# Two layers of a hybrid trunk on one core: what is worked around the last gates, and the passage from layer 0 to layer 1

## The chip, the core and the metric

The kernel runs on one core of a Trainium2 chip. A core has the engines TensorE (PE: matmuls), VectorE (DVE), ScalarE (ACT), GpSimd (POOL) and SyncE (SP, which here only issues DMAs), each with an instruction queue of its own that it works in order, and 16 DMA engines that carry all its transfers. The metric is the device time of one execution in microseconds (us).

## The reference

Two layers work on 256 latent tokens and 256 context tokens of width 1024. Layer 1 gives no context output, so its second half has 256 tokens where layer 0 has 512.

```python
def trunk_layer(x, xc, ...):
    pl = split_cols(modulate(rmsnorm(x, n1_g), sh1, sc1) @ w_in)     # and pc from xc
    ya, yb, yc = gdn_mixer(...), diff_mixer(...), natten_mixer(...)
    x = x + gt1 * merge_branches(ya, yb, yc, pl[12], w_up, w_out)
    x = x + gt2 * peer_ffn(modulate(rmsnorm(x, n2_g), sh2, sc2), p_wq, p_keys, p_u, p_v)

def peer_ffn(h, wq, keys, u, v):            # 8 heads, 128 x 128 experts, 16 kept per head
    s = einsum('thpd,hpnd->thpn', (h @ wq), keys)
    sv, si = top_k(s, 16); ...; top_s, top_pos = top_k(cand_s, 16)
    gate = softmax(top_s)                    # idx: the 16 experts of each head
    act = gelu(einsum('td,thkd->thk', h, u[idx]))
    return einsum('thk,thkd->td', gate * act, v[idx])
```

## The kernel before

The Tile framework's scheduler fixes the order in each engine's queue when the kernel is built; `tc.issue_after(x)` puts an instruction behind x. Activations are feature-major: partitions hold features, columns hold tokens. A matmul in full precision is three passes over high and low parts (`mm3`, L240 to L246); `wload` (L213) brings a weight tile by DMA, ACT makes the high part, DVE or POOL the low part.

**PEER** is worked densely over the experts, in 128 tiles by the first key's index i1. For each i1 there is a *u stage* (24 matmuls of `mm3` over the tile of u, Gelu at L1325), a product with the gates `Gt` (DVE, L1326), a split into `ah` (ACT, L1330) and `al` (DVE, L1331), and a *V stage* (`vstage`, L1294: for each block of 128 tokens six matmuls of 512 columns into PSUM banks that collect over all i1). The tiles of v are loaded and split beforehand (`vparts`, L1303 and L1305; L158 and L159). In layer 0 the 384 tokens of blocks 1 to 3 go this way, 18 matmuls in a V stage; in layer 1 256 tokens, 12 matmuls. Block 0 of layer 0 goes by gathers: POOL fetches rows of u and v by indirect DMA (L1256), DVE forms the dot products (L1262) and the sum `gacc` (L1274). `due` (L1289) deals 260 such items over the i1: from GA on, over GB tiles, twice as many for i1 below 16 and for 26 to 111 as for the others (`share`).

**The gates.** `spread` (L1198) builds the table of gates by groups c of four tokens, 96 of them in layer 0 and 64 in layer 1: DVE (one c in eight: ACT) makes one-hot matrices (L1207, L1210, L1215), PE multiplies them (L1218), ACT copies the result to `stg` (L1219). Each 32 tokens are written to `Gd` in DRAM (L1224) and read back as `Gt`, four i1 at a time (L1314). Between the groups PE gets other work: `early_tiles` (L1167) works the first 26 u tiles in plain fp32 (L1176, eight matmuls or *fills* each), eleven of them before the gates and fifteen among them, as evenly as `fill` (L1188) can spread them: 120 fills over the 96 or 64 groups.

**From layer 0 to layer 1.** The residual is written to DRAM as `xs2` (L1010) after layer 0's second norm and comes back as `xr0` (L1346). `gacc` is transposed and added at i1 = 120 (L1347); after the last V stage the sums are copied (L1364, L1366), transposed (L1371) and added (L1374). Layer 1 then takes the sums of squares (L165 to L173), normalises all 512 columns (`norm_mod`, L178 to L207) and works its first projection tiles 4, 5, ..., whose convolutions follow.

## Time and profile before

| | us |
|---|---|
| median of three runs (3756.0, 3765.81, 3756.54) | 3756.54 |
| the profiled execution: its time / its span | 3751.19 / 3749.4 |
| busy: PE, DVE, ACT, POOL | 3549.1, 2710.7, 1553.2, 988.5 |

The span is the time from the first to the last instruction in the trace. Busy times overlap, since the engines work beside each other. The granted clock of PE is 1.00 at its upper level of 2.4 GHz, and 0.50 at the lower one of 1.2 GHz; a figure between is a mean over a stretch.

### The profile page before, as it was taken

How to read it: one execution, taken by the hardware profiler on the slowest of the kernel's cores; microseconds unless marked ns; L12 is line 12 of the kernel's file. 1: busy time of each engine (PE TensorE's matmuls, PEld its weight loads, DVE VectorE, ACT ScalarE, POOL GpSimd, SP SyncE). 2: the span in 40 equal slices, each digit the busy share in tenths (PEclk: the TensorE clock that was granted, in tenths of full speed). 3: DMA queues.
4: the chain of work that ended last, by engine and by line, in shares of the span. 5: the costliest groups of instructions: out<-in, count | busy, mean ns of one | idle time of the engine just before them, and what ended most of it. 6: DMA issues, size and time to landing. Idle time of an engine off the chain costs nothing. (4 is left out here: it accounts for less than half of the span.)

```text
span 3749.4 us, 53254 instructions
## 1 busy us (share of the span) xinstructions
PE 3549.1 (95%) x19889; PEld 3052.4 (81%) x19889; DVE 2710.7 (72%) x5479; ACT 1553.2 (41%) x2454; POOL 988.5 (26%) x761
## 2 busy tenths in 40 slices
PE   7899999898999889999999989998999999999998
PEld 4788766677778679999999977887698998999997
DVE  7767556975999777777777648687567886666666
ACT  4312554224347433333333334123655475444444
POOL 3311332333300344433443212121333100222221
PEclk9989999999999999999999999799999999999999
DMA  4211123652235899888888732224245468666664
GB/s 183 97 43 33 47 76 117 219 171 94 87 135 208 318 335 317 295 296 310 291 301 300 251 115 85 74 92 162 72 148 163 146 237 265 211 211 206 216 213 132
DMA packets 265587, 681.56 MB, mean 182 GB/s; under 512 B 20976, under 2 KB 115696, under 8 KB 261744
## 3 DMA queue, kind: packets, MB, share of 16 engines
q1 hardware_dynamic: 228464, 543.93, 43.4%
q0 software_dynamic: 36864, 134.23, 10.3%
q8 instruction: 156, 2.56, 0.3%
q14 instruction: 103, 0.84, 0.1%
HBM read 626.17 MB, written 51.90 MB: 181 GB/s over the span
## 5 line engine op out<-in xcount | busy, mean ns | idle before, releaser
L246 PE MATMUL pm<-hhi,wlo 128*128 128x256 f32 (+2 forms) x2888 | 968.8, 336 | 22.0 <-DVE wlo L229 19.8
L244 PE MATMUL pm<-hhi,whi 128*128 128x256 f32 (+2 forms) x2888 | 968.9, 336 | 16.0 <-ACT whi L227 12.8
L245 PE MATMUL pm<-hlo,whi 128*128 128x256 f32 (+2 forms) x2888 | 970.4, 336 | 1.3 <-POOL hlo L207 0.9
L227 ACT CAST whi<-wr 128x1024 fp32r<-128x1024 f32 (+1 forms) x430 | 430.3, 1001 | 865.8 <-PE pm L245 672.4
L246 PEld LDWEIGHTS pm<-hhi,wlo 128*128 128x128 f32 x2888 | 554.2, 192 | 64.9 <-DVE wlo L229 26.6
L244 PEld LDWEIGHTS pm<-hhi,whi 128*128 128x128 f32 x2888 | 554.8, 192 | 61.2 <-ACT whi L227 13.6
L245 PEld LDWEIGHTS pm<-hlo,whi 128*128 128x128 f32 x2888 | 554.7, 192 | 47.4 <-issue 5.2
L232 POOL TENSOR_TENSOR wlo<-wr,whi 128x1024 fp32r<-128x1024 f32 x124 | 300.7, 2425 | 1086.6 <-ACT whi L227 1032.5
L1300 PE MATMUL ps<-vh,ah 128*128 128x512 f32 x1280 | 401.0, 395 | 22.2 <-ACT ah L1330 13.8
L1300 PE MATMUL ps<-vl,ah 128*128 128x512 f32 x1280 | 398.9, 393 | 0.9 <-DVE vl L159 0.9
L1300 PE MATMUL ps<-vh,al 128*128 128x512 f32 x1280 | 397.9, 392 | 0.2 <-DVE al L1331 0.2
L159 DVE TENSOR_TENSOR vl<-vr,vh 128x1024 fp32r<-128x1024 f32 x256 | 313.6, 1225 | 89.9 <-ACT vh L158 89.6
L232 DVE TENSOR_TENSOR wlo<-wr,whi 128x1024 fp32r<-128x1024 f32 x181 | 223.7, 1236 | 197.1 <-ACT whi L227 196.7
L158 ACT CAST vh<-vr 128x1024 fp32r<-128x1024 f32 x256 | 268.5, 1049 | 175.2 <-PE ps L1300 107.7
L1256 POOL DMA_INDIRECT gr<-in_un_dram,gix x128 | 175.5, 1371 | 476.6 <-DVE gr L1262 231.2
L1326 DVE TENSOR_TENSOR act<-act,Gt 128x384 f32<-128x384 f32 (+1 forms) x256 | 222.2, 874 | 103.8 <-ACT act L1325 91.2
L1300 PEld LDWEIGHTS ps<-vl,ah 128*128 128x128 f32 x1280 | 241.2, 189 | 56.4 <-DVE vl L159 3.6
L1300 PEld LDWEIGHTS ps<-vh,al 128*128 128x128 f32 x1280 | 241.2, 189 | 53.1 <-DVE al L1331 0.8
L1300 PEld LDWEIGHTS ps<-vh,ah 128*128 128x128 f32 x1280 | 233.4, 190 | 61.3 <-ACT ah L1330 16.5
L1330 ACT CAST ah<-act 128x384 fp32r<-128x384 f32 (+1 forms) x256 | 117.2, 459 | 385.2 <-DVE act L1326 365.6
L1176 PE MATMUL pm<-h2f,wr 128*128 128x384 f32 (+1 forms) x832 | 251.4, 433 | 2.8 <-ACT act L1179 2.8
L1256 POOL DMA_INDIRECT gr<-in_v_dram,gix x128 | 177.6, 1387 | 279.5 <-DVE gacc L1274 239.3
(386 smaller groups left out, 5619.6 us busy)
## 6 DMA issues: line engine op xcount, KB each, us to landing
wr<-in_u_dram SPq DMA_DIRECT2D x256, 512.0 KB, 4.6
vr<-in_v_dram SPq DMA_DIRECT2D x256, 512.0 KB, 4.7
wr<-in_w_in_dram SPq DMA_DIRECT2D x130, 512.0 KB, 3.6
aw<-in_ada_w_dram SPq DMA_DIRECT2D x88, 512.0 KB, 4.3
Gd<-stg SPq DMA_DIRECT2D x20, 2048.0 KB, 7.2
Gt<-Gd SPq DMA_DIRECT2D x32, 768.0 KB, 7.6
wr<-in_wq_dram SPq DMA_DIRECT2D x32, 512.0 KB, 3.5
Gt<-Gd SPq DMA_DIRECT2D x32, 512.0 KB, 4.7
```

The source lines that it names most:

```text
L158: (e_hi or ACT.copy)(hi, t)
L159: (e_lo or POOL).tensor_tensor(lo, t, hi, op=OP.subtract)
L227: ACT.copy(hi[:, :k], raw[:, :k])
L232: e.tensor_tensor(lo[:, :k], raw[:, :k], hi[:, :k], op=OP.subtract)
L244: PE.matmul(p, whi[:, i, :], xhi[:, i, c0:c1], start=st, stop=False)
L245: PE.matmul(p, whi[:, i, :], xlo[:, i, c0:c1], start=False, stop=False)
L246: PE.matmul(p, wlo[:, i, :], xhi[:, i, c0:c1], start=False, stop=sp)
L1176: e = PE.matmul(p[:, 0:TD], raw[:, k], h2f[:, k, G0:T], start=k == 0, stop=k == 7).ins
L1256: POOL.indirect_dma_start(out=r, out_offset=None, in_=src, in_offset=bass.IndirectOffsetOnAxis(ap=gix[:, j:j + 1], axis=0))
L1300: PE.matmul(acc[t][hf], x1[:, c], x2[:, 512 * hf:512 * hf + 512], start=i1 == 0 and n == 0, stop=i1 == 127 and n == 2)
L1326: DVE.tensor_tensor(a.rearrange("p (b t) -> p b t", t=TB), a.rearrange("p (b t) -> p b t", t=TB), Gt[:, :, e, :], op=OP.mult)
L1330: ACT.copy(ah, a)
```

## The change

- `PRE` gets a fourth number: three of the early u tiles in layer 0 and four in layer 1 (24 and 32 fills) no longer lie between the groups of the gates but behind the last one.
- The first two tiles of v are loaded and split with `wload` before the last 128 tokens' gates, in the buffers of the weights (low part on DVE). The last write to `Gd` is cut in two: the columns of the first eight i1, then the others.
- The gathers start at i1 = 8 (GA) where they started at 2; they end at 120 as before.
- The last three V stages (`LAST`) are put off and worked block by block of tokens at the end.
- In layer 0 each finished block passes to layer 1 token-major: `finish` adds it to the residual, takes the norm's factor and scales; `modulated` transposes it and applies shift and scale. Blocks 0 and 1 pass before layer 1's first matmul; blocks 2 and 3 pass while four projection tiles (4 to 7) are worked on columns 0 to 255, and the same tiles follow on columns 256 to 511. For it `xs2` is written token-major (32 transposes, 8 copies, 8 DMAs behind layer 0's second norm), the gate vector goes to DRAM and back as rows (`g2d`, `g2w`), and layer 1's `xs1` is written by 16 transposes, 4 copies and 4 DMAs behind the four tiles.

```diff
-GA, GB = 2, 118
+LAST = 3
+EARLY1 = ((4, "pa"), (5, "pa"), (6, "pm"), (7, "pm"))
+GA, GB = 8, 112
-PRE = ((16, 10, 11), (26, 0, 11))
+PRE = ((16, 10, 11, 3), (26, 0, 11, 4))
...
             else:
-                DVE.scalar_tensor_tensor(mg, mod[:, 8:16, :], 1.0,
...
-                ready[1, 4] = wload(w_in[1, 4])
-                norm_mod(xT, sumsq(xT, 512), npool, 512, hhi, hlo, mg, mod[:, 0:8, :])
-            if l == 1:
+                parts[:] = [wp, pool(st, "ep", 2)]
+                tiles = [(PSUM(tag), *wload(w_in[1, j])) for j, tag in EARLY1]
+                for c in (0, 256):
+                    for n, (p, whi, wlo) in enumerate(tiles):
+                        e = mm3(p[:, c:c + 256], whi, wlo, hhi, hlo, (c, c + 256))
+                        if c == 0 and n < 2:
+                            with tc.issue_after(e):
+                                modulated(2 + n, xt0[:, 2 + n],
+                                          npool.tile([128, 8, 128], F32, name=nm("nz"), tag="nz", bufs=2), "ps")
+                for (j, _), x in zip(EARLY1, tiles):
+                    early[1, j] = x[0]
+                parts[:] = [wp] * 2
                 xs_dram = dr.tile([128, 8, 256], F32, name="xs1")
-                SP.dma_start(xs_dram, xT[:, :, 0:256])
+                for t in range(2):
+                    for hf in range(2):
+                        p = PS()
+                        for k in range(4):
+                            PE.transpose(p[:, 128 * k:128 * k + 128],
+                                         xt0[:, t, 512 * hf + 128 * k:512 * hf + 128 * k + 128], ident)
+                        w = npool.tile([128, 4, 128], F32, name=nm("nt"), tag="nt", bufs=4)
+                        ACT.copy(w, p.rearrange("p (k n) -> p k n", k=4))
+                        SP.dma_start(xs_dram[:, 4 * hf:4 * hf + 4, 128 * t:128 * t + 128], w)
...
+            if l == 0:
+                xs2 = dr.tile([4, 128, 1024], F32, name="xs2")
+                for t in range(4):
+                    for hf in range(2):
+                        p = PS()
+                        for k in range(4):
+                            PE.transpose(p[:, 128 * k:128 * k + 128], xT[:, 4 * hf + k, 128 * t:128 * t + 128], ident)
+                        w = npool.tile([128, 512], F32, name=nm("nt"), tag="nt", bufs=4)
+                        ACT.copy(w, p)
+                        SP.dma_start(xs2[t, :, 512 * hf:512 * hf + 512], w)
+                g2d = dr.tile([2, 1024], F32, name="g2d")
+                for i in range(2):
+                    SP.dma_start(g2d[i].rearrange("(k p) -> p k", p=128), mod[:, 40:48, i])
         if l == 0:
-            xs2 = dr.tile([128, 8, 512], F32, name="xs2")
-            SP.dma_start(xs2, xT)
...
-                    fill(8 * NR + -(-8 * (NP - NR) * at_[2] // (TD // 4)) - at_[1])
-                SP.dma_start(Gd[(128 // TB) * t + b - G0 // TB], stg)
+                    fill(8 * NR + -(-8 * (NP - NR - NE) * at_[2] // (TD // 4)) - at_[1])
+                g = Gd[(128 // TB) * t + b - G0 // TB]
+                if at_[2] < TD // 4:
+                    SP.dma_start(g, stg)
+                else:
+                    for c in (slice(0, 2 * GS), slice(2 * GS, 128)):
+                        SP.dma_start(g[:, c], stg[:, c])
+                    fill(8 * NE)
...
+                if t == NT - 1:
+                    vready = {}
+                    for i1 in range(2):
+                        vh, vl = wload(v[l, i1].rearrange("p (k n) -> p k n", k=8), e=DVE)
+                        vready[i1] = [x.rearrange("p k n -> p (k n)") for x in (vh, vl)]
                 spread(t, rt_[t])
...
-                if i1:
+                if i1 > 0 and i1 <= 128 - LAST:
                     vstage(*acts.pop(0))
...
+                    SP.dma_start(xt0, xs2.rearrange("t p n -> p t n"))
...
+            def finish(b, parts_):
+                y, i = xt0[:, b], b // 2
+                w = dp.tile([128, 1024], F32, name=nm("gr"), tag="gr", bufs=4)
                 for hf in range(2):
+                    c = slice(512 * hf, 512 * hf + 512)
+                    DVE.tensor_tensor(w[:, c], parts_[hf], g2w[:, i, c], op=OP.mult)
+                    DVE.tensor_tensor(y[:, c], y[:, c], w[:, c], op=OP.add)
+                    ACT.activation(w[:, c], y[:, c], AF.Square, accum_out=ss[:, b, hf:hf + 1])
+                DVE.tensor_tensor(ss[:, b, 0:1], ss[:, b, 0:1], ss[:, b, 1:2], op=OP.add)
+                r = rstd_cols(dp, ss[:, b, 0:1], 1, 1.0 / D, EPS)
...
+                ACT.activation(yn[:, 0:512], y[:, 0:512], AF.Copy, scale=r)
+                DVE.tensor_scalar(yn[:, 512:1024], y[:, 512:1024], r, None, op0=OP.mult)
+                return yn
+            def modulated(b, yn, z, tag):
...
+                        last["norm"] = ACT.activation(z[:, d], p[:, 128 * k:128 * k + 128], AF.Identity, scale=mg1[:, d, i:i + 1],
+                                                      bias=mods[1][:, d, i:i + 1]).ins
+                    DVE.tensor_copy(hhi[:, h, n], z[:, h])
+                    DVE.tensor_tensor(hlo[:, h, n], z[:, h], hhi[:, h, n], op=OP.subtract)
+            for b in range(NTB + 1):
+                for x in acts if b else ():
+                    vstage(*x, ts=(b - 1,))
+                yn = finish(b, acc[b - 1] if b else [gacc[:, 0:512], gacc[:, 512:1024]])
+                if b < 2:
+                    modulated(b, yn, dp.tile([128, 8, 128], F32, name=nm("gr"), tag="gr", bufs=4), "pm")
+        else:
+            for t in range(NTB):
+                for x in acts:
+                    vstage(*x, ts=(t,))
```

The end of layer 0's gates in PE's queue, before: L1218 are the products of a group, L1176 a fill with its early tile `pm`, and L244 to L246 the u stage of i1 = 26, with which the stage of experts begins.

```order
L1218 MATMUL ps_10174<-o_2167_10181,o_2166_10175 128x128
L1218 MATMUL ps_10174<-o_2168_10184,o_2166_10175 128x128
L1218 MATMUL ps_10174<-o_2169_10187,o_2166_10175 128x128
L1218 MATMUL ps_10174<-o_2170_10190,o_2166_10175 128x128
L1176 MATMUL pm_10086<-h2f_6790,wr_10084 128x384
L244 MATMUL pm_11106<-hhi_6779,whi_11102 128x384
L245 MATMUL pm_11106<-hlo_6780,whi_11102 128x384
L246 MATMUL pm_11106<-hhi_6779,wlo_11103 128x384
```

And after, where L1249 are the products of a group, L1206 a fill, and L1344 the V stage of i1 = 0:

```order
L1249 MATMUL ps_10213<-o_2181_10223,o_2179_10214 128x128
L1249 MATMUL ps_10213<-o_2182_10226,o_2179_10214 128x128
L1249 MATMUL ps_10213<-o_2183_10229,o_2179_10214 128x128
L1206 MATMUL pm_10109<-h2f_6790,wr_10107 128x384
L1206 MATMUL pm_10240<-h2f_6790,wr_10238 128x384 x8
L1206 MATMUL pm_10253<-h2f_6790,wr_10251 128x384 x8
L1206 MATMUL pm_10266<-h2f_6790,wr_10264 128x384 x8
L1344 MATMUL ps_10289<-whi_9639,ah_10298 128x512
```

Three early tiles stand behind the last group, and the V stage follows them; the u stages of i1 = 26 and 27 that stood there now come behind the 25th V stage.

The same place in SP's queue, before: L1224 writes the last part of the gates, L221 loads u tiles, L1314 reads the gates of the first four i1, L1305 loads v tiles.

```order
L221 DMA wr_11100<-in_u_dram 128x1024
L221 DMA wr_11171<-in_u_dram 128x1024
L1224 DMA Gd_6897<-stg_10047 128x4096
L221 DMA wr_11241<-in_u_dram 128x1024
L221 DMA wr_11312<-in_u_dram 128x1024
L1314 DMA Gt_10216<-Gd_6897 128x12x128
L1305 DMA vr_10223<-in_v_dram 128x1024
L1305 DMA vr_10234<-in_v_dram 128x1024
```

And after, where L1203 and L225 load u tiles (the last of these that of i1 = 26), L1261 writes the last part of the gates in two, L1360 reads gates and L1351 loads v tiles:

```order
L1203 DMA wr_10238<-in_u_dram 128x1024
L1261 DMA Gd_6963<-stg_10090 128x256
L1261 DMA Gd_6963<-stg_10090 128x3840
L1203 DMA wr_10251<-in_u_dram 128x1024
L1203 DMA wr_10264<-in_u_dram 128x1024
L225 DMA wr_11129<-in_u_dram 128x1024
L1360 DMA Gt_10295<-Gd_6963 128x12x128
L1351 DMA vr_10330<-in_v_dram 128x1024
L1351 DMA vr_10359<-in_v_dram 128x1024
```

The first `Gt` stands behind three u tiles in place of two, and the first v tile of this stretch is that of i1 = 2.

ACT's queue at the end of layer 0, before: L1330 is the last `ah`, L1366 copies the sums, L165 and L169 square the residual's rows, L227 casts tiles of the input projection.

```order
L1325 ACTIVATE act_18109<-pm_18084 128x384
L1330 CAST ah_18112<-act_18109 128x384
L1366 COPY otm_18158<-ps_10210 128x512
L1366 COPY otm_18186<-ps_10211 128x512
L1366 COPY otm_18158<-ps_10214 128x512
L1366 COPY otm_18186<-ps_10215 128x512
L165 ACTIVATE ssq_18234<-xr_11169 128x512
L169 ACTIVATE ssq_18234<-xr_11169 128x512
L227 CAST whi_18392<-wr_18390 128x1024
L227 CAST whi_18480<-wr_18478 128x1024
L169 ACTIVATE ssq_18234<-xr_11169 128x512
```

And after, behind the scaling of block 3: L231 casts the weight tiles 5, 7, 8 and on, L1436 applies shift and scale to blocks 2 and 3, L391 copies `xs1`; the hand-over of the first projection tile to its convolution comes behind the fourth such copy.

```order
L231 CAST whi_18359<-wr_18357 128x1024
L231 CAST whi_18373<-wr_18371 128x1024
L1436 ACTIVATE nz_18401<-ps_18402,mod_64,mg_18158 128x128 x4
L1436 ACTIVATE nz_18401<-ps_18413,mod_64,mg_18158 128x128 x4
L231 CAST whi_18826<-wr_18824 128x1024
L1436 ACTIVATE nz_18448<-ps_18449,mod_64,mg_18158 128x128 x4
L1436 ACTIVATE nz_18448<-ps_18460,mod_64,mg_18158 128x128 x4
L231 CAST whi_18878<-wr_18876 128x1024
L231 CAST whi_18919<-wr_18917 128x1024
L391 COPY nt_18621<-ps_18616 128x512
L391 COPY nt_18629<-ps_18624 128x512
L391 COPY nt_18637<-ps_18632 128x512
```

The casts of tiles 5 and 7 stand ahead of the modulation of blocks 2 and 3, and four copies of `xs1` stand between the projection tiles and their convolution.

## Rows read from the trace of the kernel before

**Rows 1.** The page: span, then busy time, share and instructions of each engine.

```profile
span 3749.4 us, 53254 instructions
...
PE 3549.1 (95%) x19889; PEld 3052.4 (81%) x19889; DVE 2710.7 (72%) x5479; ACT 1553.2 (41%) x2454; POOL 988.5 (26%) x761
```

**Rows 2.** Windows: stretch, length, busy us of PE, PEld, DVE, ACT, POOL, clock, DMA.

```profile
1074.00:1237.00 163.00, 162.80 (x1007) 131.33 (x1008) 152.10 (x468) 123.20 (x170) 0.00 (x0) 1.00 0.51 190
1254.40:1350.00 95.60, 81.78 (x319) 62.98 (x320) 75.63 (x118) 27.65 (x38) 44.97 (x34) 0.92 0.97 350
1350.00:2200.00 850.00, 848.93 (x4274) 769.79 (x4273) 616.71 (x747) 306.46 (x411) 304.09 (x218) 1.00 0.83 289
```

**Rows 3.** Timeline of PE, last gates of layer 0: start, us, engine, line, operation.

```profile
1234.39 1.05 PE L1218 MATMUL ps<-o,o 128*128 128x128 f32 x8
1235.28 0.81 PE L1176 MATMUL pm<-h2f,wr 128*128 128x384 f32 x2
1235.92 1.05 PE L1218 MATMUL ps<-o,o 128*128 128x128 f32 x8
...
1254.38 1.65 PE L1300 MATMUL ps<-vh,ah 128*128 128x512 f32 x3 [8.43 <-ACT vh L158]
```

**Rows 4.** Timeline of SP's queue at the same place.

```profile
1238.12 0.33 SPq L1224 DMA_DIRECT2D Gd<-stg  x1
1238.55 3.41 SPq L221 DMA_DIRECT2D wr<-in_u_dram  x2
1245.43 0.38 SPq L1314 DMA_DIRECT2D Gt<-Gd  x1
```

**Rows 5.** Waits of PE from 1230 to 1350: total us, times, longest.

```profile
PE ps L1300 <- ACT ah L1330: 12.7, 5, 5.3
```

**Rows 6.** Lines from 1350 to 2200: operands, count, busy us and mean ns, idle before.

```profile
L159 DVE TENSOR_TENSOR vl<-vr,vh 128x1024 fp32r<-128x1024 f32 x109 | 133.6, 1226 | 15.5 <-ACT vh L158 15.4
...
L1262 DVE SCALAR_TENSOR_TENSOR gr<-gr,htm 128x1024 f32<-128x1024 f32 x95 | 115.8, 1219 | 1.8 <-DMA gr<-in_un_dram,gix 1.8
...
L1326 DVE TENSOR_TENSOR act<-act,Gt 128x384 f32<-128x384 f32 x106 | 58.4, 552 | 0.0
...
L1331 DVE TENSOR_TENSOR al<-act,ah 128x384 fp32r<-128x384 f32 x107 | 59.7, 558 | 56.3 <-ACT ah L1330 56.2
```

**Rows 7.** Timeline of PE and ACT at the end of layer 0.

```profile
2216.90 0.63 PE L1300 MATMUL ps<-vh,ah 128*128 128x512 f32 x2
...
2222.35 1.07 ACT L1366 COPY otm<-ps 128x512 f32<-128x512 f32 x2 [3.63 <-PE ps L1300]
...
2225.10 3.03 PE L1371 MATMUL ps<-cst,otm 128*128 128x128 f32 x24
...
2244.27 1.87 PE L173 MATMUL ps<-cst,ssq 128*128 128x1 f32 x8 [16.14 <-DVE ssq L170]
...
2251.18 1.22 PE L244 MATMUL pm<-hhi,whi 128*128 128x512 f32 x2 [2.37 <-DVE hhi L206]
```

**Rows 8.** Windows: first convolutions of layer 1.

```profile
2265.00:2325.00 60.00, 56.35 (x282) 46.56 (x280) 47.55 (x85) 25.92 (x41) 10.65 (x18) 0.94 0.31 97
```

**Rows 9.** Windows: layer 0's second norm, and behind it.

```profile
895.00:907.20 12.20, 5.07 (x14) 2.53 (x15) 10.41 (x23) 11.08 (x20) 5.11 (x3) 0.50 0.57 204
907.20:930.00 22.80, 22.80 (x105) 18.58 (x105) 13.42 (x82) 8.66 (x12) 10.09 (x10) 0.93 0.16 52
```

**Rows 10.** The page, DMA queue: packets, MB, share of 16 engines.

```profile
q1 hardware_dynamic: 228464, 543.93, 43.4%
```

**Rows 11.** Windows: gates of layer 1.

```profile
2975.00:3083.00 108.00, 108.00 (x748) 101.87 (x747) 103.05 (x309) 83.01 (x119) 2.77 (x1) 1.00 0.58 211
```

**Rows 12.** Timeline of PE behind those gates.

```profile
3096.31 0.58 PE L244 MATMUL pm<-hhi,whi 128*128 128x256 f32 x1 [6.75 <-ACT whi L227]
```

**Rows 13.** Windows: a later stage of layer 1.

```profile
2402.00:2447.00 45.00, 45.00 (x207) 40.58 (x206) 22.22 (x48) 4.12 (x12) 3.04 (x2) 0.51 0.12 36
```

More of the change, by code (lines that the diff above doesn't have):

```diff
@@ L245, in mm3 @@
             PE.matmul(p, whi[:, i, :], xlo[:, i, c0:c1], start=False, stop=False)
-            PE.matmul(p, wlo[:, i, :], xhi[:, i, c0:c1], start=False, stop=sp)
+            e = PE.matmul(p, wlo[:, i, :], xhi[:, i, c0:c1], start=False, stop=sp)
+        return e.ins
     ready, early = {}, {}
@@ L291, in third @@
             parts.append(p)
-        hhi, hlo = new_h()
-        mg = cp.tile([128, 8, 2], F32, name=f"mg{l}")
+        if l == 0:
+            hhi, hlo = new_h()
+            mg = cp.tile([128, 8, 2], F32, name=f"mg{l}")
         with ExitStack() as st:
@@ L992, in hybrid_trunk @@
         NBK = TD // TB
-        NA, NX, NR = PRE[l]
+        NA, NX, NR, NE = PRE[l]
         NP = NA + NX
@@ L1181, in early_tiles @@
                     yield e
+        GS = 4
         fills = early_tiles()
@@ L1292, in due, with vstage @@
             return -(-ntodo * sum(share[GA:GA + i]) // sum(share[GA:GA + GB]))
-        def vstage(i1, ah, al, vh, vl):
+        def vstage(i1, ah, al, vh, vl, ts=range(4)):
             for t in range(NTB):
+                if t not in ts:
+                    continue
                 c = slice(128 * t, 128 * t + 128)
@@ L1303, in vparts @@
         def vparts(i1):
+            if i1 in vready:
+                return vready.pop(i1)
             vr = dp.tile([128, 1024], F32, name=nm("vr"), tag="vr", bufs=3)
@@ L1343, in hybrid_trunk @@
                     ux_st.close()
-                    xst = ExitStack()
-                    xT = pool(xst, "xp", side="right").tile([128, 8, 512], F32, name=f"xr{l}")
-                    SP.dma_start(xT, xs2)
-            if G0 and g == 30:
-                for hf in range(2):
-                    p = PM()
+                    xe_st = ExitStack()
+                    xe = pool(xe_st, "xe", side="right")
+                    xt0 = xe.tile([128, 4, 1024], F32, name="xt0")
+                    SP.dma_start(xt0, xs2.rearrange("t p n -> p t n"))
@@ new lines, in hybrid_trunk @@
+                    g2w = xe.tile([128, 2, 1024], F32, name="g2w")
+                    for i in range(2):
+                        SP.dma_start(g2w[:, i], g2d[i:i + 1].to_broadcast([128, 1024]))
+        if l == 0:
+            hhi, hlo = new_h()
+            mg1 = cp.tile([128, 8, 2], F32, name="mg1")
+            DVE.scalar_tensor_tensor(mg1, mods[1][:, 8:16, :], 1.0,
+                                     vcol(1, 0, 8).unsqueeze(2).to_broadcast([128, 8, 2]), op0=OP.add, op1=OP.mult)
+            ss = xe.tile([128, 4, 2], F32, name="xss")
+            with tc.issue_after(last["gelu"]):
+                ACT.activation(ss[:, 0, 0:1], ones[:, 0:1], AF.Sqrt)
+            def finish(b, parts_):
+                y, i = xt0[:, b], b // 2
+                w = dp.tile([128, 1024], F32, name=nm("gr"), tag="gr", bufs=4)
+                for hf in range(2):
+                    c = slice(512 * hf, 512 * hf + 512)
[4 more added lines that the diff above has]
+                r = rstd_cols(dp, ss[:, b, 0:1], 1, 1.0 / D, EPS)
+                yn = dp.tile([128, 1024], F32, name=nm("gr"), tag="gr", bufs=4) if b < 2 else y
+                ACT.activation(yn[:, 0:512], y[:, 0:512], AF.Copy, scale=r)
+                DVE.tensor_scalar(yn[:, 512:1024], y[:, 512:1024], r, None, op0=OP.mult)
+                return yn
+            def modulated(b, yn, z, tag):
+                i = b // 2
+                n = slice(128 * b, 128 * b + 128)
+                for hf in range(2):
+                    p = PSUM(tag)
@@ L1350, in hybrid_trunk @@
                     for k in range(4):
[L1351 removed]
+                        PE.transpose(p[:, 128 * k:128 * k + 128], yn[:, 512 * hf + 128 * k:512 * hf + 128 * k + 128],
                                      ident)
+                    h = slice(4 * hf, 4 * hf + 4)
                     for k in range(4):
                         d = 4 * hf + k
[L1355 to L1356 removed]
@@ L1357, in hybrid_trunk @@
-        vstage(*acts.pop(0))
-        if l == 0:
-            for hf in range(2):
-                otm = dp.tile([128, NTB, 512], F32, name=nm("otm"), tag="otm")
-                for t in range(NTB):
-                    if t == 1:
-                        DVE.tensor_copy(otm[:, t], acc[t][hf])
-                    else:
-                        ACT.copy(otm[:, t], acc[t][hf])
-                for k in range(4):
-                    d = 4 * hf + k
-                    p = PS()
-                    for t in range(NTB):
-                        PE.transpose(p[:, 128 * t:128 * t + 128], otm[:, t, 128 * k:128 * k + 128], ident)
-                    for s in range(NSTR):
-                        c0, c1 = max(G0, 256 * s), 256 * s + 256
-                        DVE.scalar_tensor_tensor(xT[:, d, c0:c1], p[:, c0 - G0:c1 - G0], mod[:, 40 + d, s:s + 1],
-                                                 xT[:, d, c0:c1], op0=OP.mult, op1=OP.add)
+                        last["norm"] = ACT.activation(z[:, d], p[:, 128 * k:128 * k + 128], AF.Identity, scale=mg1[:, d, i:i + 1],
+                                                      bias=mods[1][:, d, i:i + 1]).ins
```

12 lines of the change are left out of this document (3 added, 9 removed).

## The prediction

> **What bounds the kernel now.** The page comes first: PE is busy for 3549 of 3749 us [rows 1], so a gain must come out of some 200 us in which PE idles, or out of stretches in which it works at its lower clock. The windows, read stage by stage, show where those lie. In layer 0's gates PE is busy for 162.8 of 163 us, with DVE close behind at 152.1; behind the gates 95.6 us hold only 81.8 us of PE work at a mean clock of 0.92; then 850 us run without a gap [rows 2]. At the end of layer 0 PE waits 16.1 us in one piece [rows 7]. The waits name the releasers: ACT's `ah` behind the gates, at the end of a chain that runs through DVE [rows 5], and the v tile before the first V stage [rows 3]. The change touches exactly these places.
>
> A pair of V matmuls takes its price from the 36 between 2216.90 and 2225.10 [rows 7]: 8.2 us, so a V stage of 18 takes 4.1 us. A fill takes 0.64 us (1235.28 to 1235.92), a group with one fill 1.53 us [rows 3].
>
> **Part 1, gates of layer 0.** 24 fills of 0.64 leave: PE's work falls by 15.4 us, from 163 to 147.6. DVE keeps its 152.1 us [rows 2] and gets the low parts of two v tiles, 2 x 1.23 [rows 6], so 154.5. The gates thus become DVE's, and PE idles about 7 us in them. Behind them stand 15.4 us of fills in place of the wait of 8.4 us for the v tile [rows 3]. Do they cover the way through DRAM? `Gd` was issued at 1238.12 and `Gt` at 1245.43, since it waits for the whole write, behind 3.4 us in which SP stood at u tiles [rows 4]. Now the first piece is a sixteenth of the columns, but `Gt` stands in SP's queue behind the load of u tile 26, whose buffer comes free when the second of the three early tiles is worked, 16 x 0.64 = 10.3 us behind the gates. From the issue of `Gt` to the first V stage the old trace has 9.0 us (1245.43 to 1254.38), the v tile's share included; without it I take 8. So V starts at 18.3, and PE idles 3 us behind its 15.4 us of fills. Idle before 8.6, now 7 + 3 = 10: cost 1.5 us. Bounds: if DVE's own waits shrink, the gates take some 150 us, a gain of 4; if the gates keep their 163 us because a group is paced by its chain and not by DVE's sum, the cost is 15.4 + 3 - 8.6 = 10.
>
> **Part 2, later gathers.** From 1254.4 to 1350 PE did 319 matmuls, nearly all of V stages [rows 2]: 17.7 stages, 72.6 us at 4.1. The stretch lost 23 us. Why: u tiles 0 to 27 are already worked, so an i1 lasts only 4.1 us on PE, while DVE needs 1.23 + 0.55 + 0.56 = 2.34 us for the v tile, the gates' product and `al`, and 1.22 for each gathered row [rows 6]. 260 items over a sum of shares of 218 are 2.39 items an i1 (share 2 below 16): 5.26 us, 1.16 too many in each of 14 i1, or 16 us; the rest is the start, with DMA at 0.97 of its time. With GA = 8 the sum is 206, 2.52 items, 5.41 us, 1.3 too many in each of 8 i1: 10.5 us. Three buffers for v let DVE run two stages ahead, 8.2 us, which it can gather in the first eight i1, where it has 1.8 us to spare in each. So the loss lies between 2.3 and 10.5 us, and with the DMAs' start I take 10. Gain 13; bounds 4 and 20. The main loop pays nothing: with a u stage (24 matmuls of 384 columns, as many columns as a V stage) an i1 lasts 8.2 us, and DVE's sum rises from 6.5 to 6.65; DVE had 617 of 850 us there and DMA 0.83.
>
> **Part 3, from layer 0 to layer 1.** Between the last V stage (2225.10) and the first projection matmul (2251.18) lie 26.1 us with 5 us of PE work [rows 7]: 21 idle. Now the last 54 V matmuls go block by block, so block 1's sums are final two blocks of 18 (8.2 us) before the end, and its chain hides under them; blocks 2 and 3 hide under the four first halves, half of four tiles of 24 x 0.228, 11 us. PE's own work hardly changes: 32 + 16 transposes at 3.03 / 24 = 0.126 come, 24 + 8 and the sums over partitions (3 us) go. I leave 5 us of idle time for the last block's chain and for ACT, where the casts of tiles 5 and 7 stand ahead of the modulation of blocks 2 and 3; PE gains 16. But the convolutions behind are DVE's as much as PE's: 47.6 and 56.4 of 60 us [rows 8], and four copies of `xs1` stand on ACT ahead of their start. So not all of it arrives: gain 11; bounds 3 and 18.
>
> **Part 4, second norm of layer 0.** 32 transposes (4.0 us on PE) and 8 copies (1.07 / 2 each, 4.3 us on ACT [rows 7]) stand ahead of the first query tile, where ACT is busy for 11.1 of 12.2 us [rows 9]. They run partly beside each other: 4 us, and 1 for what follows late. `g2d` writes 2048 single numbers. A packet of SP's queue took 0.434 x 3749.4 x 16 / 228464 = 0.114 us [rows 10], so these take 14.6 us of all 16 DMA engines, beside a stretch with a DMA share of 0.16 [rows 9]: covered. Cost 5; bounds 1 and 8. The Trainium skill, page "DMA: Bandwidth & Descriptors", section "Specifications", says that transfers under 512 bytes miss the line rate because the engine reads, changes and writes back. By that rule such a packet may cost twice the mean, 29 us beside query tiles, and this part would come to 8, still within its bounds; no row here shows single numbers apart.
>
> **Part 5, gates of layer 1.** 32 fills of 256 / 384 x 0.64 = 0.43 us move: PE falls from 108 to 94.3 us, DVE stands at 103 and gets 2.5 [rows 11]. PE idles 11 us in the gates and about 1 behind, where it waited 6.75 [rows 12] and some smaller times. That is a cost of 5; DVE's 103 hold waits, so I take 3, between a gain of 3 and a cost of 8.
>
> **Part 6, the end.** Put off by block, the sums of the first 128 tokens are final three half stages (4.1 us) before the last matmul in place of one: at most 2.7 us, since the last block's chain stays. Gain 1.5; bounds 0 and 2.7.
>
> **Sum.** -1.5 + 13 + 11 - 5 - 3 + 1.5 = 16 us. The profiled execution took 3751.2, so 3735.2; the median of the runs is 5.3 above it: 3740.5, rounded to 3740.
>
> **Rivals.** (a) *The passage gives nothing*: ACT's queue and DVE's convolutions set the time behind the seam, and PE's 16 us come back as waits there. DVE's 47.6 of 60 us speak for it; that PE was the fuller engine speaks against. 3740 + 11 = 3751. (b) *The gathers' loss only moves*: DVE cannot run ahead, since the DMAs at 0.97 hold back v tiles, and i1 8 to 15 lose all of 10.5 us plus the start's 10. Gain 3: 3750. (c) *A stretch at the lower clock goes*: from 2402 to 2447 PE is busy without a break at a clock of 0.51 [rows 13]. Nothing in the change names this stage, but its arrival shifts. At the upper level the same work would take half: 3740 - 22 = 3718. For it: the loop of the experts holds 1.00 [rows 2], so work without a break can. Against: small matmuls, the same before and after. (d) *Slower: the clock falls in the gates.* Today PE is full there at its upper level [rows 2]. With the fills gone it has a gap in every group, and a lower clock then makes PE the late engine. The stretch behind the gates, with 14% gaps, had 0.92, a sixth of its time at the lower level. A sixth of both gates' 260 us is 43 us, each costing half of itself: 21 us, 3761; at twice the share 3782; I price it at 3770. It turns the result when more than 33 us are at the lower level. Against it: the gaps would be 5 to 10%, some 0.1 us in each group, not waits of 5 us as there [rows 5]. The Trainium skill states the mechanism in "TensorE: Matmul & The Clock Gate", section "HAM oscillation — how this bites in real kernels": bursts of matmuls with waits between them let the clock drop again and again. The trace agrees for the stretch with waits of 5 us; of gaps as short as these it has no case.
>
> **How the numbers follow.** Forecast 0.52, own range 3728 to 3750; (a) 0.14; (b) 0.10; (c) 0.14; (d) 0.10. The bounds of the parts added up at their ends would give 3710 to 3776 for the forecast alone; they will not all fall to one side. The range reaches to (c) and past (a) and leaves out most of (d): 3714 to 3762. What a measurement of this kernel can tell from no change is 0.3%, 11.3 us. Faster (under 3745): 0.41 of the forecast, 0.13 of (c), 0.04 of (a) and (b): 0.58. Slower (over 3768): 0.08 of (d) and 0.01 elsewhere: 0.09. Same: 0.33.
>
> **What would show it.** Part 1: PE 90 to 96% busy in the gates with DVE at its limit, and the first V stage released by `Gt`'s chain. Part 2: no idle PE in the first eight V stages and some 10 us in the next eight. Part 3: a wait under 6 us where 16.1 stood, the clock at 1.00, and waits on DVE or ACT in the convolutions. Part 4: some 5 us more between the norm and the first query tile. Part 5: idle PE in layer 1's gates, none behind. I am wrong if the gates keep 163 and 108 us, if the loss at the gathers stays above 15 us, or if the time to the first convolution shrinks by less than 3 us.

## The result, and the profile after

The changed kernel takes 3798.66 us (median of six runs, 3789.45 to 3806.91), the kernel before 3756.27 beside it (3745.78 to 3765.81). The ratio is 1.0112, interval 1.0092 to 1.0132: some 42 us slower, where I had forecast 16 faster, and above the range. The profiled execution of after took 3806.91, the longest of its six.

The page of after, span and busy times [rows 1]:

```profile
span 3805.1 us, 53628 instructions
...
PE 3582.7 (94%) x20021; PEld 3081.8 (81%) x20021; DVE 2703.3 (71%) x5483; ACT 1563.6 (41%) x2494; POOL 984.2 (26%) x758
```

The span grew by 55.7 us, PE's busy time by 33.6. The 132 matmuls more are small, so part of that is the same work at PE's lower clock (1.2 GHz; a clock of 1.00 in the rows is 2.4): the mean granted clock was 0.958 over this span and 0.966 over that of before. The stages, cut at the first and last PE instruction of each in the profiled executions of before, of after, and of after without its early v tiles (an experiment below), us:

| Stage | before | after | without v tiles |
|---|---|---|---|
| layer 0 up to its up-projection, not edited | 616.7 | 624.1 | 621.6 |
| up-projection; second norm; to the gates | 457.5 | 465.1 | 465.0 |
| gates of layer 0 | 162.5 | 161.2 | 149.3 |
| from there to the last V matmul | 988.2 | 995.3 | 990.2 |
| last V matmul to layer 1's convolved keys and values | 128.8 | 141.4 | 141.6 |
| layer 1's mixers, not edited | 386.3 | 394.1 | 363.1 |
| layer 1: up-projection to gates | 234.5 | 238.0 | 236.3 |
| gates of layer 1, to the last V matmul | 763.0 | 774.4 | 767.1 |

The gates of layer 0, their tail, the first V stages and the experts' loop behind them, windows of after (columns as in [rows 2], which they answer):

```profile
1089.00:1250.60 161.60, 150.57 (x959) 122.77 (x960) 151.10 (x469) 121.92 (x168) 0.00 (x0) 0.97 0.51 188
1250.60:1280.40 29.80, 18.87 (x51) 10.34 (x49) 1.16 (x3) 3.35 (x7) 3.96 (x4) 0.81 0.73 251
1280.40:1350.00 69.60, 66.55 (x278) 53.86 (x279) 57.74 (x90) 26.80 (x38) 23.34 (x18) 0.96 0.97 328
1350.00:2200.00 850.00, 848.94 (x4265) 768.67 (x4264) 633.18 (x769) 306.36 (x411) 327.54 (x234) 1.00 0.87 300
```

PE's work in the gates did shrink, but 11 of their 161.6 us are now idle. PE's timeline there shows one piece of it, and the tail behind the gates [rows 3]:

```profile
1189.34 1.05 PE L1249 MATMUL ps<-o,o 128*128 128x128 f32 x8
1201.25 1.65 PE L1206 MATMUL pm<-h2f,wr 128*128 128x384 f32 x2 [10.86 <-DMA wr<-in_u_dram]
1202.69 1.79 PE L1249 MATMUL ps<-o,o 128*128 128x128 f32 x8
1204.32 0.81 PE L1206 MATMUL pm<-h2f,wr 128*128 128x384 f32 x2
...
1250.47 5.97 PE L1206 MATMUL pm<-h2f,wr 128*128 128x384 f32 x18
1260.68 13.03 PE L1206 MATMUL pm<-h2f,wr 128*128 128x384 f32 x32 [4.24 <-DMA wr<-in_u_dram]
1280.46 1.22 PE L1344 MATMUL ps<-whi,ah 128*128 128x512 f32 x2 [6.75 <-ACT ah L1376]
```

PE stands 10.86 us at a u tile in the middle of the gates. The rows behind that wait take 1.65 and 1.79 us where the same rows take 0.81 and 1.05: it also cost the clock. SP's queue shows why the u tile came late [rows 4]:

```profile
1177.40 0.33 SPq L1257 DMA_DIRECT2D Gd<-stg  x1
1177.82 13.45 SPq L225 DMA_DIRECT2D wr<-in_v_dram  x2
1191.32 0.42 SPq L1257 DMA_DIRECT2D Gd<-stg  x1
1191.85 5.95 SPq L1203 DMA_DIRECT2D wr<-in_u_dram  x2
...
1251.74 0.80 SPq L1261 DMA_DIRECT2D Gd<-stg  x2
1252.66 4.15 SPq L1203 DMA_DIRECT2D wr<-in_u_dram  x2
...
1273.74 0.38 SPq L1360 DMA_DIRECT2D Gt<-Gd  x1
```

The v tiles are loaded by `wload`, into the same two raw buffers as the u tiles. The first row with `in_v_dram` holds both loads: the first issued at 1177.82, the second at its end, 13 us later. Behind them in the queue stand the write of `Gd` and the u tile that PE is to work next (1191.85). ACT and DVE show what the second load waited for:

```profile
1187.20 1.04 ACT L231 CAST whi<-wr 128x1024 fp32r<-128x1024 f32 x1
```

```profile
1189.63 1.29 DVE L236 TENSOR_TENSOR wlo<-wr,whi 128x1024 fp32r<-128x1024 f32 x1
```

A raw buffer is free once ACT's cast and DVE's low part have read it, and DVE's stands in order behind the gates' own work. So the second v load was issued when DVE ended the first low part (1190.9). Then came the u tile's turn, and it took 9.4 us to land beside the 2048 KB of `Gd` just issued: PE went on at 1201.25.

The passage to layer 1, SP's queue [rows 7 and 8 show the place in before]:

```profile
2220.24 63.09 SPq L225 DMA_DIRECT2D wr<-in_w_in_dram  x9
2284.68 2.58 SPq L392 DMA_DIRECT2D xs<-nt  x4
2287.30 1.19 SPq L400 DMA_DIRECT2D row<-in_rows_dram  x1
```

PE at the end of the V stages and at the first projection matmul:

```profile
2245.41 0.62 PE L1344 MATMUL ps<-vh,al 128*128 128x512 f32 x2
2245.86 1.06 PE L1431 MATMUL pm<-cst,gr 128*128 128x128 f32 x8
2248.60 0.38 PE L248 MATMUL pa<-hhi,whi 128*128 128x256 f32 x1 [1.68 <-DVE hhi L1438]
```

and DVE and ACT at the start of the convolutions, with the first copy `pad` of before as the last row:

```profile
2293.26 0.29 DVE L834 TENSOR_TENSOR lm<-row 128x128 f32<-128x128 f32 x1 [7.70 <-DMA row<-in_rows_dram]
2293.47 0.88 DVE L482 TENSOR_SCALAR cva<-pad,vec 128x512 f32<-128x512 f32 x2
```

```profile
2284.07 2.05 ACT L391 COPY nt<-ps 128x512 f32<-128x512 f32 x4 [2.35 <-PE ps L388]
2285.98 1.12 ACT L479 COPY pad<-pa 128x512 f32<-128x512 f32 x2
```

```profile
2265.11 0.58 ACT L460 COPY pad<-pm 128x512 f32<-128x512 f32 x1
```

The last V matmul ends at 2245.9 and the first projection matmul follows at 2248.60, 2.7 us behind it, where 26 us lay in before [rows 7]. But the first convolution's copy `pad` starts at 2285.98, 40.1 us behind the last V matmul: in before it was 40.0 (2265.11). PE, early with the projection, waited for that copy:

```profile
PE pm L248 <- ACT pad L479: 19.1, 1, 19.1
```

DVE waited 7.7 us more for a row of constants, whose load SP issues behind nine weight loads and four stores of `xs1`.

The mixers of layer 1, which no edit touches, differ by the clock. Windows of the bulk of that stage in before, in after and in after without v tiles:

```profile
2353.00:2740.00 387.00, 359.29 (x2217) 303.44 (x2215) 273.02 (x543) 136.72 (x278) 86.26 (x74) 0.90 0.30 97
```

```profile
2399.80:2781.00 381.20, 356.30 (x2138) 301.14 (x2139) 256.42 (x525) 133.79 (x271) 77.25 (x65) 0.87 0.29 91
```

```profile
2380.00:2740.00 360.00, 333.40 (x2212) 280.76 (x2212) 259.14 (x530) 136.11 (x278) 83.71 (x68) 0.97 0.31 100
```

With two levels, one half of the other, a mean clock c over a length L means 2 x (1 - c) x L at the lower one: 77, 99 and 22 us.

### The profile page after: what moved, and what is told of

Its sections match the earlier page's. It is cut to its first block, busy times and chain, and to the rows that moved or that the text cites. A ratio compares the mean times of both kernels' runs of the same rounds, so it can differ in the third digit from the quotient of the medians.

```text
span 3805.1 us, 53628 instructions
## 1 busy us (share of the span) xinstructions
PE 3582.7 (94%) x20021; PEld 3081.8 (81%) x20021; DVE 2703.3 (71%) x5483; ACT 1563.6 (41%) x2494; POOL 984.2 (26%) x758
## 4 chain that ended last, share of the span: by engine, by line
PE 70%; DVE 8%; issue 3%; DMA 3%; ACT 2%; POOL 1%; SPq 0%; DVEq 0%; POOLq 0%; ACTq 0%
PE ps L1344 20%; PE pm L250 11%; PE pm L249 11%; PE pm L248 11%; PE pm L1206 5%; PE ps L1249 4%; PE ps L618 1%; DVE ajk L133 1%; PE ps L612 1%; DMA wr<-in_u_dram 1%; DVE aw L133 1%; PE py L936 1%; DVE wlo L233 1%; PE pa L811 1%; PE ps L1096 1%
## 5 line engine op out<-in xcount | busy, mean ns | idle before, releaser
L231 ACT CAST whi<-wr 128x1024 fp32r<-128x1024 f32 (+1 forms) x434 | 434.5, 1002 | 891.3 <-PE pm L249 708.4
L1344 PE MATMUL ps<-vl,ah 128*128 128x512 f32 x1260 | 390.9, 391 | 4.8 <-DVE vl L163 4.8
L1344 PE MATMUL ps<-vh,ah 128*128 128x512 f32 x1260 | 391.5, 392 | 0.2 <-ACT vh L162 0.2
L1344 PE MATMUL ps<-vh,al 128*128 128x512 f32 x1260 | 389.7, 390 | 0.0
L1344 PEld LDWEIGHTS ps<-vl,ah 128*128 128x128 f32 x1260 | 235.8, 188 | 59.6 <-DVE vl L163 8.3
L1206 PE MATMUL pm<-h2f,wr 128*128 128x384 f32 (+1 forms) x832 | 257.7, 441 | 22.1 <-DMA wr<-in_u_dram 19.3
L1344 PEld LDWEIGHTS ps<-vh,al 128*128 128x128 f32 x1260 | 236.5, 188 | 51.2
L1344 PEld LDWEIGHTS ps<-vh,ah 128*128 128x128 f32 x1260 | 228.6, 188 | 36.0 <-ACT vh L162 0.6
L234 POOL TENSOR_TENSOR wlo<-wr,whi 128x512 fp32r<-128x512 f32 (+1 forms) x97 | 157.4, 1624 | 352.2 <-ACT whi L231 348.2
```

Source lines behind the costliest of these rows:

```text
L231: ACT.copy(hi[:, :k], raw[:, :k])
L234: e.tensor_tensor(lo[:, k // 2:k], raw[:, k // 2:k], hi[:, k // 2:k], op=OP.subtract)
L1206: e = PE.matmul(p[:, 0:TD], raw[:, k], h2f[:, k, G0:T], start=k == 0, stop=k == 7).ins
L1344: PE.matmul(acc[t][hf], x1[:, c], x2[:, 512 * hf:512 * hf + 512], start=i1 == 0 and n == 0, stop=i1 == 127 and n == 2)
```

## The experiments

All ratios are to the kernel before, run beside on the same chip; 0.3% is 11.3 us.

| Run | us | before beside it | ratio, 95% interval |
|---|---|---|---|
| gath_only | 3746.07 | 3756.99 | 0.9970 (0.9949 to 0.9991) |
| tiles_only | 3762.92 | 3756.99 | 1.0011 (0.9990 to 1.0032) |
| gates_only | 3787.83 | 3756.99 | 1.0091 (1.0062 to 1.0120) |
| seam_only | 3771.89 | 3756.99 | 1.0035 (1.0018 to 1.0052) |
| after_nov | 3752.62 | 3757.63 | 0.9993 (0.9976 to 1.0010) |
| seam_row | 3764.78 | 3757.63 | 1.0025 (1.0008 to 1.0042) |
| seam_mend | 3764.47 | 3757.63 | 1.0030 (1.0009 to 1.0050) |
| best | 3756.18 | 3757.63 | 0.9997 (0.9981 to 1.0014) |
| after_vown | 3761.76 | 3756.10 | 1.0017 (1.0002 to 1.0032) |
| best2 | 3752.20 | 3756.10 | 0.9994 (0.9980 to 1.0008) |
| after_shift | 3808.31 | 3756.10 | 1.0135 (1.0110 to 1.0161) |
| before_shift | 3756.91 | 3756.10 | 1.0009 (0.9992 to 1.0026) |
| seam_two | 3749.49 | 3756.24 | 0.9980 (0.9967 to 0.9993) |
| gath_l0 | 3748.92 | 3756.24 | 0.9972 (0.9956 to 0.9989) |

**One part at a time.** First the later gathers alone, in the kernel before.

```diff
-GA, GB = 2, 118
+GA, GB = 8, 112
```

> The kernel before with one number pair changed: gathers start at i1 = 8 (GA, GB = 8, 112). Theory G (the V-only stretch behind the gates is bound by DVE and DMA, and starting later takes the loss away): 12 to 16 us faster than before, the stretch from the first V stage to the last shorter by as much. Rival (the loss only moves to i1 8 to 15): within 4 us of before.

Faster by 11 us, interval 3 to 19. In its trace PE's waits from 1250 to 1450 are

```profile
PE ps L1300 <- ACT vh L158: 12.9, 2, 8.2
PE ps L1300 <- DVE vl L159: 7.3, 5, 3.7
```

The waits for `ah` of before [rows 5] are gone. But those for v tiles are 20.2 us, with 9.3 in before (8.4 of them in [rows 3]), and this one profile shows the stage up to the last V matmul only 2.6 us shorter (985.6 us), near rival (b)'s gain of 3. That the kernel got faster is shown. That more than 2.6 of the 11 us come from the gathers is not: the median granted clock of its runs was 0.967, with 0.964 in before beside it, and stages that no edit touches run with the clock (below).

Then the tiles kept for the end of both gates, with `Gd`'s last write in two pieces, without and with the early v tiles:

```diff
-PRE = ((16, 10, 11), (26, 0, 11))
+PRE = ((16, 10, 11, 3), (26, 0, 11, 4))
```

> The kernel before with only the early tiles moved behind the last gates (three in layer 0, four in layer 1) and the last write to Gd in two. Theory S (SP's queue and two raw buffers: the moved fills run at the pace of their loads, and the first Gt is issued only when the last fill is done): the gates of layer 0 shrink to 150 to 154 us, but the first V stage comes 30 us or more behind them; the whole 15 to 25 us slower than before. Rival D (the gates keep their time, a group is paced by its own chain): gates 160 us or more even without the v tiles, the whole 25 to 35 us slower. Third: what was lost in the full change came from the v tiles alone, then within 6 us of before.

```diff
+                if t == NT - 1:
+                    vready = {}
+                    for i1 in range(2):
+                        vh, vl = wload(v[l, i1].rearrange("p (k n) -> p k n", k=8), e=DVE)
```

> As the one with only the early tiles moved, and the first two v tiles loaded through the weights' buffers ahead of the last gates. Theory S: an 11 us stall of the fills inside layer 0's gates (SP waits for the low part of the first v tile), part of it won back since the first V stage has its v tile; in all 25 to 35 us slower than before, 5 to 12 slower than without the v tiles. Rival: the v tiles pay, faster than the one without them.

Tiles alone: no difference that can be told; the gates fall to 149.3 and 99.9 us, and in layer 0 what they give comes back behind them (1002.2 us to the last V matmul, 988.2 in before). With the v tiles: slower by 34 us, and the gates stay at 161.9 us. Its PE waits in 1080 to 1260:

```profile
PE pm L1176 <- DMA wr<-in_u_dram: 15.1, 2, 10.8
```

That is the wait of after. tiles_only has only a wait of 4.2 us for a u tile, behind the gates; so the v tiles cause it.

The passage alone is after with `GA` and `NE` set back, the last write to `Gd` whole and no v tiles; Part 4's edits and the put-off V stages stay in it.

> The changed kernel without its parts around the gates and with the old start of the gathers: only the passage between the layers (and what it needs in layer 0's second norm) is new. Theory P (the convolutions start no earlier, and the pair of PSUM banks held by tiles 6 and 7 keeps PE waiting until ACT copies them): 12 to 20 us slower than before, 4 of it in layer 0's second norm. Rival (the loss at the seam came from the other parts, through memory and queue order): faster than before by 5 to 10 us.

Slower by 13 us. Gathers -11, gates +34 and passage +13 add up to 36 of the 42 us. In its profiled execution the loss is not in the passage's own stage alone (143.8 us, 128.8 in before): the stage with the second norm took 465.3 us for 457.5, and that from the gates to the last V matmul 998.5 for 988.2, while the mixers ran 366.7 for 386.3. Why the V stages lose 10 us there was not followed.

**The v tiles, taken out or given buffers of their own.**

```diff
-                    for i1 in range(2):
+                    for i1 in range(0):
```

> The changed kernel without the early loads of the first two v tiles. Theory V (these two loads, through the two raw buffers of the weights, cost some 30 us: SP stalls, the fills in the gates starve, and nothing is won at the first V stage): 25 to 35 us faster than the changed kernel, 0 to 10 us slower than the kernel before; layer 0's gates at 149 us, where the changed kernel had 161. Rival (the parts don't add up, the loads hide behind other stalls in the full change): less than 12 us faster than the changed kernel.

46 us come off. The window of its layer 0 gates:

```profile
1089.00:1237.00 148.00, 147.99 (x947) 119.67 (x946) 145.67 (x458) 119.73 (x166) 0.00 (x0) 1.00 0.53 196
```

PE is full again, at the upper clock. Between the two profiled executions, the longest of after and one of after_nov below its median (3747.34 us), lie 59.5 us of span: 17 of them in layer 0's gates and V loop, 7 in layer 1's, and 31 in the mixers, at another clock (below).

```diff
+                        vx = sp2.tile([128, 8, 128], F32, name=nm("vx"), tag="vx", bufs=2)
+                        SP.dma_start(vx, v[l, i1].rearrange("p (k n) -> p k n", k=8))
```

> The changed kernel with the two early v tiles loaded into buffers of their own in place of the two raw buffers that the early u tiles use. Theory V (the shared raw buffers starve the fills): no wait of PE for a u tile inside layer 0's gates, gates at 150 to 153 us where the changed kernel had 161, the whole 10 us or more faster than the changed kernel. Rival (the v tiles cost through DVE and DMA wherever they lie): gates stay at 158 or more.

The v tiles stay where after has them, with their casts and low parts, but no longer in the u tiles' buffers: 37 us below after. The gates take 151.1 us, 10 less than in after, and no u tile is waited for inside them. (Of the 45 us between the two profiled executions 28 lie in the untouched mixers, at another clock; so not all of the 37 are shown to be the buffers'.) What is left behind them in PE's timeline is that of after:

```profile
1237.31 5.97 PE L1206 MATMUL pm<-h2f,wr 128*128 128x384 f32 x18
1247.50 13.25 PE L1206 MATMUL pm<-h2f,wr 128*128 128x384 f32 x32 [4.22 <-DMA wr<-in_u_dram]
1267.46 0.79 PE L1348 MATMUL ps<-whi,ah 128*128 128x512 f32 x1 [6.71 <-ACT ah L1380]
```

So the shared buffers are the cause of the wait in the gates, not ACT's and DVE's work on the tiles. And ready v tiles win about 1 us: from the gates to the first V stage this kernel takes 30.3 us, after 30.1, after_nov 31.2. The wait is for `Gt`, as DVE's first product with the gates shows in after:

```profile
1279.24 1.50 DVE L1372 TENSOR_TENSOR act<-act,Gt 128x384 f32<-128x384 f32 x3 [31.20 <-DMA Gt<-Gd]
```

**The passage, mended wait by wait.** First the row of constants loaded ahead of the weights, then also `xs1`'s copies and stores put between the two half passes; best adds `GA, GB = 8, 112`.

```diff
+                row1 = cp.tile([128, 272], F32, name="row1")
+                SP.dma_start(row1, bass.AP(tensor=rows.tensor, offset=rows.offset + 272, ap=[[0, 128], [1, 272]]))
```

> The kernel with only the new passage between the layers, with one load moved: the row of constants that layer 1's gates need is loaded at the start of the program, not behind nine weight loads and the stores of xs1. Theory R (DVE's queue stands still for 7.7 us on this load, ahead of the convolutions): 4 to 8 us faster than the passage alone, no wait on row in the trace. Rival (the convolutions then wait for something else): within 3 us.

> As the one with the row loaded early, and the transposes, copies and stores of xs1 stand between the first and the second halves of the four projection tiles, not behind them. Theory X (ACT's hand-over to the first convolution waits for the xs1 copies, which wait for all four tiles): the first convolution starts 15 to 19 us earlier behind the last V stage than in the passage alone, the whole 12 to 18 us faster than it, 0 to 5 us faster than before. Rival (DVE's convolutions are the bound wherever they start): the start moves, but the whole gains under 6 us on the passage alone.

> The mended passage with the later gathers (GA, GB = 8, 112), the gates as in the kernel before. If the parts add up: 10 to 18 us faster than before. Rival: the loads of the token-major residual behind the gates meet the later gathers, then no faster than before.

With the row early, the time from the last V matmul to the first sums for the keys' norm falls from 60.3 to 51.2 us, what it is in before (52.6), and the passage's stage from 143.8 to 130.2 (128.8 in before). With `xs1` moved it is 52.2, and DVE has a new wait at the same place:

```profile
DVE cva L488 <- POOL pad L483: 11.1, 1, 11.1
```

None of the three is faster than before.

I took POOL's memsets of the pad's borders for the next cause. best2 puts them on DVE, and loads the residual later:

```diff
+                ms = DVE if l else POOL
+                ms.memset(pad[:, :, 0:2], 0.0)
+                ms.memset(pad[:, :, 258:260], 0.0)
```

> The mended passage with later gathers, and two more edits: in layer 1 the zeros of the convolutions' borders are written by DVE, not by POOL, whose queue stands behind a load; and the token-major residual is fetched at i1 = 60, not 26. Theory Q (the passage is held by one in-order queue after the other): from the last V stage to the first norm of the convolutions 40 to 44 us where the mended passage had 52; the V stages 5 to 10 us shorter; the whole 10 to 18 us faster than the mended passage with later gathers. Rival: DVE's convolutions hold the time, under 5 us.

That theory fell: 52.6 us, and the memset itself waits for the projection.

```profile
DVE pad L484 <- PE pm L250: 6.5, 1, 6.5
```

The memory of the convolutions' buffers is, by this wait, that of the four tiles' weights, and is free only when all four are worked. So I let two tiles go ahead, not four, without the second pool (`ep`) in which the four had part of their weights:

```diff
-EARLY1 = ((4, "pa"), (5, "pa"), (6, "pm"), (7, "pm"))
+EARLY1 = ((4, "pa"), (5, "pa"))
```

> The mended passage (row early, xs1 between the halves, border zeros on DVE) with two projection tiles worked ahead, not four; later gathers; the moved early tiles in layer 0 alone, without the v tiles. Theory M (the buffers of the convolutions lie where the weights of the tiles worked ahead lay, so no convolution starts before the last of these tiles is done, some 38 us behind the last V stage with four): with two tiles the first convolution starts 28 to 32 us behind the last V stage, the time from there to the first norm falls from 52 to 42 to 46 us; the whole 15 to 25 us faster than before. Rival (DVE's convolutions and the late blocks hold the time): still 50 us or more, within 10 us of before.

> The kernel before with the later gathers and three early tiles moved in layer 0 alone: no v tiles, the old passage, layer 1 as before. If part 1 without its v tiles costs nothing and part 2 gains, 8 to 15 us faster than before, layer 0's gates at 149 us. Rival: the moved tiles give back what the gathers gain, within 4 us of before.

seam_two, which also keeps late tiles in layer 0 and loads the residual where after does, is faster than before by 0.2%. Its first convolution stands some 25 us behind the last V matmul. The way to the keys' sums is 38.2 us, 14 less than in before; but up to the last of the convolved keys and values it is 123.8 against 128.8: 9 of the 14 go again. PE's longest waits in that stretch:

```profile
PE ps L272 <- ACT hsq L270: 6.4, 2, 4.8
PE ps L510 <- DVE cva L507: 3.2, 2, 2.1
```

ACT's squares and DVE's convolutions now come late; which of them holds the 9 us was not tried apart. Nor were the two edits, fewer tiles and one pool less. gath_l0 has the gathers and layer 0's late tiles with the old passage: 10.5 us faster by the ratio. It, seam_two and gath_only can't be told apart by their intervals.

**The clock in the mixers.** Theory: the time at which that stage is reached sets how long it runs at the lower clock. Sixteen matmuls whose result is not used shift it, in before behind the last V stage, in after ahead of the three that are put off:

```diff
+            p = PM()
+            for _ in range(16):
+                PE.matmul(p, h2h[:, 0, 0:128], h2h[:, 0, 0:512], start=True, stop=True)
```

> The changed kernel with 16 matmuls of 512 columns more (3.6 us, their result unused) behind the last V stage of layer 0. Theory C (in layer 1's mixers the clock falls to its lower level for a time that depends on when the kernel arrives there): the time at the lower clock in layer 1's mixers changes by 20 us or more from the 99 us of the changed kernel, and the whole moves by more than 6 us, most likely down, though work is added. Rival (the time at the lower clock belongs to the stage's own instructions): 4 us slower, 90 to 105 us at the lower clock.

> The kernel before with the same 16 matmuls behind its last V stage. Theory C: the time at the lower clock in layer 1's mixers differs by 20 us or more from the 75 us of the kernel before, either way. Rival: 4 us slower, 70 to 80 us at the lower clock.

after_shift has some 109 us at the lower clock there against 99, before_shift some 55 against 77. The first speaks against the theory, the second changes too little to carry it. The runs say the same: the median granted clock is 0.960 in after and in after_shift, 0.965 in before_shift and in before beside it. What puts this stage at some 20 us in one profile and at 99 in another stays open; each is a single execution. The 116 runs of before beside the experiments go from 3732.40 us at a clock of 0.972 to 3770.77 at 0.961, so executions of one kernel differ too. The kernels differ as well: the runs of after (0.958 to 0.964) and of after_nov (0.968 to 0.973) do not overlap.

## Why the prediction was wrong

**Parts 1 and 3 failed, and with them the sign.** By stages, Parts 1 and 2 missed by 17 us (they cost 5.8, where 11.5 were to be gained), Part 3 by 24 and Part 5 by 8; without the v tiles the kernel is still no faster than before (0.9993). Another 18.7 us lie in three stages that no part priced: layer 0 up to its up-projection, the mixers, and the stage behind them. The median granted clock of after's runs is 0.960, that of before's 0.964: some 33 us more at the lower level, so by an estimate some 17 of the 42 us go with the clock, in whatever stage.

**Part 1.** Its step "the low parts of two v tiles, 2 x 1.23" priced the work and not the way: the loads go through the u tiles' two buffers and SP's queue, whose order I had followed for `Gt` only. The 5.8 us that it cost together with Part 2, which shares its stages, are -1.3 in the gates and +7.1 behind. Layer 1 has the same defect. By the medians, the v tiles cost 46 us (after against after_nov) or 25 (gates_only against tiles_only); in the stages that they touch, the gates and the V loops of both layers, 24 and 22. Without them the gates took 148 us, PE's own sum of 147.6; DVE's 145.67 did not bound them, as I had forecast that it would. The way to the first V stage was mis-sized too, 30 us and not 18.3. SP issued `Gt` at 1273.74, just when the last fill ended, a wait that SP's record puts down to the fills. In the code the pool `dp`, which holds `Gt`, opens where the fills' input `h2f` closes, so I take shared memory for the reason; no run moved it.

**Part 2 is half shown**: gath_l0, which is Parts 1 and 2 without v tiles, gained 10.5 us by its ratio (4 to 17) and 11.5 in its stages, the number forecast for the two. That is in part luck: its gates take 149.3 us, where I had 154.5, and the stage behind them is 1.7 us longer than in before. Alone, the later gathers gave 2.6 of their 13 us in that stage. In after, PE's waits from 1280 to 1480 are

```profile
PE ps L1344 <- ACT ah L1376: 6.7, 1, 6.7
PE ps L1344 <- DVE vl L163: 4.1, 6, 1.5
```

The first is the start; 4.1 us for v tiles stand where I had allowed 10.

**Part 3 was wrong**, and rival (a) right and too mild. Its step from "PE gains 16" to "gain 11" had the projection matmuls early, 2.7 us behind the last V matmul. But the convolutions started where they had (40.1 and 40.0 us), and to their end the passage cost 12.6 us instead of giving 11. The causes stood in a row. Loading the row of constants early gave 9 us. Moving the four copies of `xs1`, which I had named, gave none: a wait for the convolutions' memory stood there, under the four tiles' weights. With two tiles ahead, and one pool less, 14 us are won against before, and 9 of them are lost again behind, at ACT and DVE. What the passage cost ahead of the last V matmul, 10 us in seam_only's profile, was not priced at all.

**Part 4 was right in its place**: from the last projection matmul ahead of the norm to the first query tile lie 22.1 us (899.92 to 922.01) where 17.5 lay (889.30 to 906.84), 4.6 more; forecast 5. The 7.6 us over its three stages hold 3.2 more in the up-projection, which no edit touches. `g2d` landed in 11.8 us a half. The Trainium skill's rule for transfers under 512 bytes ("DMA: Bandwidth & Descriptors", "Specifications") had given 8, with the cost beside the query tiles. The trace does not show that cost: from the first query tile to the gates it has 167.2 us, before 167.4. No run took `g2d` alone away.

**Part 5**: 11.4 us against 3; without v tiles 4.1. The defect is that of Part 1. In after PE waits 3.6 us for a u tile there, and the early v tiles leave its wait behind the gates at 5.19 us [rows 12 had 6.75].

**Part 6** gave nothing that the stages show; forecast 1.5.

**Rival (d)**, the clock in the gates, was not the mechanism, for the gaps it needed did not come: without v tiles PE was busy for 147.99 of 148 us, at 1.00. Where the wait of 10.86 us stands, it was 0.97 over the gates, with the slow rows right behind. The Trainium skill, "TensorE: Matmul & The Clock Gate", "HAM oscillation — how this bites in real kernels", has the clock fall at waits for data; the trace with that wait agrees.

**Rival (c)**, a stretch at the lower clock, came both ways: in layer 1's mixers 77 us of it in before, 99 in after, 22 in after_nov. The stage follows it: 386.3, 394.1 and 363.1 us. So no sum made on one profile could be right to 10 us. Of the 46 us between after and after_nov some 20 may be this and not the wait; that they belong to the v tiles is not shown.

## What to carry to other kernels

A load that is moved ahead is priced by the buffers and the in-order queue that it passes, not by the work on its data: ask which buffer it takes, who must read that buffer before the next load, and which instructions stand behind that load. Before a stage is given an earlier start, follow its first instruction on every engine, its constants and the memory that its buffers inherit; one wait mended only shows the next. Read a gain of one per cent by stages, and put the time at the lower clock on an account of its own.

## What the runs showed of the hardware that was not expected

In sixteen profiled executions, one of each kernel, the same untouched stage (layer 1's mixers) ran some 20 to 109 us at the lower clock and took 363 to 398 us. The shortest time belongs to the least of it, the longest to the most (after_nov and after_shift). Within one kernel, too, the time of a run goes with its mean granted clock: after's six runs go from 3789.45 us at 0.964 to 3806.91 at 0.958, and the 116 of before from 3732.40 at 0.972 to 3770.77 at 0.961.
